# A pooling-mixer layer on one core: one product of the second input phase computed as seven products

## The chip, the cores and the metric

One Trainium2 chip, one of its cores. The metric is the device time of one execution in microseconds (us), measured on that core. Before the change three runs gave 906.58, 906.6 and 907.85 us; the median is 906.6.

Engines as the profile names them: PE is TensorE (matmuls), PEld its weight loads, DVE is VectorE, ACT is ScalarE, POOL is GpSimd, SP is SyncE, which issues most DMAs.

## What is computed

One layer of a streaming trunk on 4096 frames of 1024 channels, in float32:

```python
def pool_mixer(h, in_w, group_w, group_b, scale, out_w):
    b, s, _ = h.shape
    u, gate = jnp.split(h @ in_w, 2, axis=-1)
    ug = u.reshape(b, s, POOL_GROUPS, POOL_GROUP_DIM)
    pooled = jnp.stack([trailing_mean(ug[:, :, g], w) for g, w in enumerate(POOL_WINDOWS)],
                       axis=2) - ug
    mixed = jnp.einsum('bsgc,gcd->bsgd', pooled, group_w) + group_b
    y = mixed.reshape(b, s, POOL_WIDTH) * scale * jax.nn.silu(gate)
    return y @ out_w

normed = rms_norm(h, norm_w[i])
h = h + pool_mixer(normed, pool_in_w[j], pool_group_w[j], ...)
return rms_norm(h, final_norm_w)
```

The four trailing windows are 2, 4, 8 and 16 frames. Nearly all of the work is two matrix products, 4096 x 1024 by 1024 x 2048 (input) and 4096 x 1024 by 1024 x 1024 (output). The group maps are multiplied into the input weights at the start.

## The kernel before

**Products by seven.** Each large product is cut in 2 x 2 blocks and done as seven block products instead of eight (the Strassen-Winograd form). The seven are called P1 to P7. P1, P2 use blocks as they are; P3 to P7 use sums and differences of blocks. Shared partial results stay in PSUM: the eight banks are two sets of four, `x` (banks 0 to 3, also called `v`) and `y` (banks 4 to 7). `bank_of` says which product adds into which set: P1, P2, P7, P4 into `x`/`v`, P6, P5, P3 into `y`.

**Three matmuls for one.** Float32 precision is had from three matmuls of a reduced type: every operand is split in a high part (a copy by ScalarE) and a low part (a subtraction by VectorE, `split`), and `mm3` (line 689) multiplies high by high, high by low and low by high.

**Phases.** The order of products is the list `steps`: the first input phase ("a", 4 blocks of 1024 frames x 7 products) makes one half of the input channels, the second ("b", again 4 x 7) the other half, the out phase ("o", 8 blocks of 512 frames x 7 smaller products) the output. An input product (`product_in`) is 2 x 4 x 2 x 3 = 48 matmuls of 512 columns, with the weights as stationary and the tokens as moving operand. Order in "b": P1, P2, P6, P7, P5, P4, P3. In the out phase eleven products (blocks 2 to 7 of P2, 2 to 6 of P4) are already done as seven products of half the size each (`inner_first`, `inner_rest`, matmuls of 256 columns at line 824, quarter sums added by VectorE at line 832, copies of a quarter bank by ScalarE); their sums of weights come from `inner_rights`, their sums of tokens from `inner_sums`.

**What happens around a product.** The loop at the end goes through `steps`. For step n it loads the blocks of step n + 3 (`load_reach`), forms sums for step n + 2 (`form`), splits the operands of step n + 1 into the four `op` tiles (`split_step`), runs pooling that is due (`pool_due`), and then runs the product and empties its banks (`run`, `evict_in`). The instructions of one engine are put in an order that need not be that of the code: an instruction whose inputs come late lets later ones past it, unless `issue_after` ties it. Emptying in phase "b": P1 is copied to the `y` banks, P2, P6, P7 and P3 are copied to SBUF by ScalarE, P5 and P4 are added there by VectorE. Where two of the four results of a block are there (after P4, after P3), `pool_later` puts the pooling of two channel groups on a list, one or two steps on; it is VectorE work (scans at line 916, scaling and subtraction at 938, bias and gate at 943 and 946) with a store to DRAM (`yd`) at its end.

**Tiles.** Work tiles are 11 `st` and 8 `vt` tiles of 512 KB. A released tile goes to the end of a free list and the oldest is taken; `keep` is the number of `vt` tiles held back for results. When blocks can be loaded depends on when these tiles come free.

**Names that the change touches.** `store_weights` / `inner_rights` / `make_wo` prepare output weights during blocks 1 and 2 of "b"; `split_wb` splits the "b" weights into `w[P3]` and so on (P3's behind block 0's P2); `split_in` splits a product's token blocks; `evict_in` empties its banks; `pool`, `pool_later`, `pool_due` do the pooling.

Of the kernel before, what the change touches and what calls it, by code (L numbers as in the profile page):

```python
# [2 lines left out]

# [7 lines left out]
F32 = mybir.dt.float32  # L11
F32R = mybir.dt.float32r
# [3 lines left out]
P = 128  # L16
# [13 lines left out]
FIRST_INNER = 2  # L30
INNER = {2: (2, 7), 4: (2, 6)}

P1, P2, P3, P4, P5, P6, P7 = range(1, 8)
# [5 lines left out]
class Slots:  # L39
# [41 lines left out]
    def retire(self):  # L81
        return self.free.popleft()[1]


@with_exitstack
def kernel(
# [51 lines left out]
    def new_st(i):  # L138
# [4 lines left out]
    st = Slots([new_st(i) for i in range(NS)])  # L143
    vt = Slots(
        [mem.tile([P, 2 * (HIST + H)], F32, tag=f"vt{i}", name=f"vt{i}") for i in range(NV)]
    )

# [164 lines left out]
    def store_weights(dst, h, b11, b21, b12, b22):  # L312
        nc.sync.dma_start(out=dst[P1][h], in_=b11)
        nc.sync.dma_start(out=dst[P2][h], in_=b21)
        if P2 in firsts:
            inner_rights(P2, b21)
        for i, u in combine(b11, b21, b12, b22).items():
            nc.sync.dma_start(out=dst[i][h], in_=u)
            if i in firsts:
                inner_rights(i, u)  # L320
            give(u)
# [58 lines left out]
    def split_wb(i):  # L380
        for h in range(2):
            (u,) = parts.pop((i, h)).values()
            if i == P1:
                split_scaled(w[i][h], u, pair(norm_c, h, 0))
            elif i == P2:
                split_scaled(w[i][h], u, pair(norm_c, h, 1))
            else:
                split(w[i][h], u)
            if i != P6:
                give(u)  # L390

    QW = H // 4

    def inner_rights(i, low):

        high = firsts.pop(i)
        more = take()
        b11, b12, b21, b22, t4, t2 = (
            u.rearrange("p k (s a) -> p k s a", s=2)[:, :, :, c * QW : (c + 1) * QW] for u in (high, low, more) for c in range(2)
        )  # L400
        sub(b11, b12, b11)
        sub(b12, b22, b12)
        sub(t2, b22, b11)
        sub(t4, b21, t2)
        for n, u in enumerate((high, more)):
            nc.sync.dma_start(out=wid[i][n], in_=u)
            give(u)

    firsts = {}

    def make_wo(h):
        if h:
            for i in INNER:
                firsts[i] = take()
                nc.sync.dma_start(out=firsts[i], in_=wod[i][0])
# [232 lines left out]
    def split_in(q, b, i):  # L648
# [8 lines left out]
        if i == P6 and swapped(q, b):  # L657
            for u in s.pop("21"):
                give(u)
        elif i not in (P1, P2, P6) and not (i == P7 and swapped(q, b)):  # L660
            for u in s.pop(key):
                give(u)
        return t

    stores = []
# [29 lines left out]
    def product_in(i, t, sets, by_bank, between=None, behind=None):  # L695
# [17 lines left out]
        if between and 8 in between:  # L713
            between[8]()

    def product_out(i, t, sets, last, between=None):
# [164 lines left out]

    def pool(b, q, half, vs, sgs):

        first = b == 0 and half == 1
        last = b == NB - 1 and half == 0
        end = HIST + H
        for g in range(2):
            grp = 2 * q + g
# [43 lines left out]
            if win > 2:  # L932
                if first:
# [21 lines left out]
            if not q:  # L955
                give(sg)
        if q:
# [12 lines left out]
    def evict_in(b, q, i, sets):  # L970
# [322 lines left out]
    def run(n, between=None, behind=None):  # L1293
# [12 lines left out]
        else:  # L1306
            product_in(i, split_up.pop(n), sets, i == P1 and n > 0, between, behind)
            evict_in(b, 0 if kind == "a" else 1, i, sets)
# [3 lines left out]
    def pool_later(n):  # L1312
# [7 lines left out]
        else:  # L1320
            return
        pending.append((n + wait, args))

# [218 lines left out]
    def load_reach(kind, b, i):  # L1542
        return 3 if kind == "a" and i == P6 else 4 if kind == "o" else 3

# [17 lines left out]

    scales = {}

# [159 lines left out]
```

## Time and profile before

| what | value |
|---|---|
| median of three runs | 906.6 us |
| the profiled execution | 906.77 us |
| its span, first to last instruction | 904.9 us |
| TensorE busy | 897.3 us, 4428 matmuls |
| VectorE busy | 766.6 us, 945 instructions |
| ScalarE busy | 480.6 us, 791 instructions |
| GpSimd busy | 38.0 us |
| mean granted TensorE clock | 0.998 of full |
| moved by DMA | 194.88 MB |

Busy time is the time in which an engine has an instruction at work; starts and lengths in the views are in us from the first instruction. In a row of a group, the numbers behind the bar are busy time, mean ns of one instruction, and idle time ahead of them with what ended it. A busy share is an average over the whole span; what a stage is limited by is read from the chain of waits in that stage.

### The profile page before, as it was taken

The page shows a single profiled execution, that of the slowest core. Times are in us where ns is not written, and L with a number is a line of the kernel's source. Part 1 is how long each engine was busy: PE and PEld are TensorE (multiplying, and loading weights), DVE is VectorE, ACT ScalarE, POOL GpSimd, SP SyncE. Part 2 cuts the span into 40 slices and gives each one's busy share as a digit, 9 for nine tenths or more (in the row PEclk, how much of TensorE's full clock was granted, in tenths as well). Part 3 has the DMA queues.
Part 4 walks back from the last instruction along what each step waited for, and adds up shares of the span by engine and source line. Part 5 has one row for each costly group of instructions (what it writes and reads, how often), then busy time and mean ns, then how long its engine had stood idle before and what let it go on. Part 6 is the DMA issues. An engine that isn't in the chain of part 4 may idle for free.

```text
span 904.9 us, 11891 instructions
## 1 busy us (share of the span) xinstructions
PE 897.3 (99%) x4428; PEld 792.6 (88%) x4428; DVE 766.6 (85%) x945; ACT 480.6 (53%) x791; POOL 38.0 (4%) x73
## 2 busy tenths in 40 slices
PE   9999999999999999999999999999999999999997
PEld 7888888888888888888888888888888998999996
DVE  5899993894998997586689499889999989889897
ACT  6879547447346555245455544754355445355354
POOL 0023201101100000000000000000000000000000
PEclk9999999999999999999999999999999999999999
DMA  9985965756856635016614774954984483584642
GB/s 348 408 318 163 344 214 205 253 192 221 294 207 229 222 133 209 24 47 233 256 46 175 283 283 167 310 178 176 316 275 155 159 314 131 196 271 162 219 186 93
DMA packets 71881, 194.88 MB, mean 215 GB/s; under 512 B 6608, under 2 KB 29008, under 8 KB 71824
## 3 DMA queue, kind: packets, MB, share of 16 engines
q1 hardware_dynamic: 65328, 172.87, 53.4%
q10 hardware_dynamic: 4176, 13.65, 4.0%
q0 software_dynamic: 2320, 7.62, 2.4%
q8 instruction: 34, 0.56, 0.3%
q14 instruction: 23, 0.19, 0.1%
HBM read 124.89 MB, written 69.22 MB: 215 GB/s over the span
## 4 chain that ended last, share of the span: by engine, by line
PE 98%; DVE 1%; ACT 0%; issue 0%; DVEq 0%; ACTq 0%
PE bank L689 89%; PE bank L824 6%; PE bank L472 3%; PE bank L1332 0%; DVE w L188 0%; DVE op L188 0%; DVE st L188 0%; PE bank L538 0%; ACT vt L1143 0%; DVE st L1223 0%; ACT vt L1184 0%; ACT vt L202 0%; ACT columns L1166 0%; DVE st L1195 0%; DVEq L1720 0%
## 5 line engine op out<-in xcount | busy, mean ns | idle before, releaser
L689 PE MATMUL bank<-op,w 128*128 128x512 f32 x2688 | 581.3, 380 | 0.1
L689 PEld LDWEIGHTS bank<-op,w 128*128 128x128 f32 x2688 | 509.2, 190 | 71.7 <-ACT early L202 0.6
L689 PE MATMUL bank<-w,op 128*128 128x512 f32 (+1 forms) x1092 | 237.0, 377 | 0.0
L689 PEld LDWEIGHTS bank<-w,op 128*128 128x128 f32 x1092 | 203.6, 190 | 27.0 <-issue 0.2
L188 DVE TENSOR_TENSOR op<-st,op 128x1024 fp32r<-128x1024 f32 x121 | 147.1, 1220 | 71.7 <-ACT op L202 71.4
L202 ACT ACTIVATE op<-st 128x1024 fp32r<-128x1024 f32 x121 | 126.9, 1052 | 101.5 <-PE bank L689 82.2
L202 ACT ACTIVATE vt<-bank 128x512 f32<-128x512 f32 x100 | 57.0, 593 | 54.3 <-PE bank L689 39.5
L202 ACT ACTIVATE op<-vt 128x1024 fp32r<-128x1024 f32 x56 | 58.5, 1052 | 44.7 <-PE bank L689 26.5
L188 DVE TENSOR_TENSOR op<-vt,op 128x1024 fp32r<-128x1024 f32 x56 | 67.9, 1219 | 6.9 <-ACT op L202 6.7
L202 ACT ACTIVATE bank<-bank 128x512 f32<-128x512 f32 (+1 forms) x70 | 35.7, 512 | 62.6 <-PE bank L689 32.0
L188 DVE TENSOR_TENSOR st<-st,st 128x1024 f32<-128x1024 f32 (+1 forms) x58 | 64.3, 1128 | 3.4 <-ACT st L293 1.2
L1223 DVE TENSOR_TENSOR vt<-bank,vt 128x512 f32<-128x512 f32 x58 | 39.4, 685 | 3.2 <-PE bank L689 3.2
L188 DVE TENSOR_TENSOR st<-st,vt 128x1024 f32<-128x1024 f32 (+1 forms) x37 | 42.0, 1161 | 0.0
L188 DVE TENSOR_TENSOR vt<-bank,vt 128x512 f32<-128x512 f32 x50 | 33.0, 686 | 6.3 <-PE bank L689 6.3
L188 DVE TENSOR_TENSOR vt<-vt,vt 128x1024 f32<-128x1024 f32 (+1 forms) x32 | 36.7, 1151 | 0.2
L824 PE MATMUL bank<-w,op 128*128 128x256 f32 x264 | 36.6, 275 | 0.0
L824 PEld LDWEIGHTS bank<-w,op 128*128 128x128 f32 x264 | 34.7, 192 | 1.2
L916 DVE TENSOR_TENSOR_SCAN vt<-vt,bf 128x512 f32<-128x512 f32 x28 | 34.5, 1271 | 1.1 <-ACT vt L202 1.1
L188 DVE TENSOR_TENSOR w<-st,w 128x1024 fp32r<-128x1024 f32 (+1 forms) x28 | 30.6, 1105 | 5.5 <-ACT w L202 5.4
L202 ACT ACTIVATE w<-st 128x1024 fp32r<-128x1024 f32 (+1 forms) x28 | 26.6, 960 | 15.9 <-PE bank L689 10.8
L202 ACT ACTIVATE st<-bank 128x512 f32<-128x512 f32 x30 | 17.6, 596 | 26.5 <-PE bank L689 17.1
L1077 POOL TENSOR_SCALAR oms<-oss 128x2 f32<-128x2 f32 x14 | 5.2, 370 | 622.3 <-ACT vt L1104 487.6
(125 smaller groups left out, 662.0 us busy)
## 6 DMA issues: line engine op xcount, KB each, us to landing
st<-in_x SPq DMA_DIRECT2D x29, 512.0 KB, 5.1
vt<-in_x SPq DMA_DIRECT2D x28, 512.0 KB, 5.2
st<-sd SPq DMA_DIRECT2D x28, 512.0 KB, 5.1
st<-in_xt SPq DMA_DIRECT2D x27, 512.0 KB, 7.5
sd<-st ACTq DMA_DIRECT2D x21, 512.0 KB, 4.7
out<-vt SPq DMA_DIRECT2D x19, 512.0 KB, 3.3
yd<-vt SPq DMA_DIRECT2D x18, 512.0 KB, 2.7
st<-yd SPq DMA_DIRECT2D x16, 512.0 KB, 5.5
```

What stands on the lines that cost most here:

```text
L188: made.append(nc.vector.tensor_tensor(out=dst, in0=a, in1=b, op=op))
L202: made.append(nc.scalar.activation(dst, src, func, **how))
L472: latest[0] = nc.tensor.matmul(ps2[kk][:, j * 256 : (j + 1) * 256], a[:, kk, 2 * j + t, :], maps if len(pairs) == 1 else woven(maps), star ...
L689: latest[0] = nc.tensor.matmul(ps, a, b, start=start and n == 0, stop=stop and n == 2, skip_group_check=True).ins
L824: latest[0] = nc.tensor.matmul(dst, a[k][x_], b[k][y_], start=start and k + n == 0, stop=k == 1 and n == 2, skip_group_check=True,).ins
L916: nc.vector.tensor_tensor_scan(s[:, j, at:end], v[:, j, at:end], v[:, j, at - win : end - win], sums_of[j] if sums_of else 0.0, ALU.add, A ...
L1077: nc.gpsimd.tensor_scalar(out=ms, in0=ss, scalar1=-0.5 / D, scalar2=-0.5 * EPS, op0=ALU.mult, op1=ALU.add)
L1223: partial["added"] = nc.vector.tensor_tensor(out=dst, in0=src, in1=dst, op=ALU.add).ins
```

## The change

Block 0 of the second input phase does its last product, P3, as seven products of half the size in each direction (`INNER_IN = (0,)`). P3 is weights (A) times tokens (B) and adds into the `y` banks. The parts are A11 B11, A12 B21, S1 T1, S2 T2, S3 T3, S4 B22 and A22 T4, S and T being sums of quarters of A and B. Three of the seven belong to one quarter of the result each and are added in the `y` banks; A11 B11, S2 T2, S3 T3 and S1 T1 are shared between quarters. The shared ones are computed in the `x` banks, which P4, the product ahead, has just left; ScalarE copies a half bank to go on from it, and VectorE adds the finished half banks to the results in SBUF, twelve additions of 256 elements.

```diff
+    def mm_inner_in(left, right, banks_, n, start):
+        a = inner_left_w[left]
+        for c in range(2):
+            for k in range(2):
+                for m, (x_, y_) in enumerate(((0, 0), (0, 1), (1, 0))):
...
+                        latest[0] = nc.tensor.matmul(
+                            quarter_bank(banks_[c], n), a[:, x_, k, c * P : (c + 1) * P],
+                            right[:, y_, k], start=start and k + m == 0,
...
+    def product_inner(t, sets):
+        r, tags = t
+        y, x = sets["y"], sets["x"]
+        in_turn[0] = None
+        mm_inner_in("A22", r["T4"], y[2:4], 0, False)
+        mm_inner_in("A11", r["B11"], x[2:4], 0, True)
+        for c in range(2):
+            copy(quarter_bank(x[c], 0), quarter_bank(x[2 + c], 0))
+        mm_inner_in("A12", r["B21"], y[0:2], 0, False)
+        mm_inner_in("S2", r["T2"], x[0:2], 0, False)
+        for c in range(2):
+            copy(quarter_bank(x[c], 1), quarter_bank(x[c], 0))
+        mm_inner_in("S4", r["B22"], y[0:2], 1, False)
+        mm_inner_in("S3", r["T3"], x[0:2], 1, False)
+        mm_inner_in("S1", r["T1"], x[2:4], 1, True)
+        for tag in tags:
+            restore(tag)
+
+    def add_shared(us, sets):
+        x = sets["x"]
...
+        for c in range(2):
+            into(c, 1, quarter_bank(x[c], 0))
+        for c in range(2):
+            for n in range(2):
+                latest_add = into(2 + c, n, quarter_bank(x[c], 1))
+        drained.append(latest_add)
+        for c in range(2):
+            into(c, 0, quarter_bank(x[2 + c], 0))
+            for m in range(2):
+                into(2 * m + c, 1, quarter_bank(x[2 + c], 1))
```

The sums. `keep_sums` makes the weights' sums behind block 0's P6, from P3's raw weights, which `split_wb` now holds back instead of releasing them. `token_sums` makes those of the tokens when P3's blocks are split, ahead of P4. Each makes four sums of 512 elements and four splits; three splits each go into work tiles taken from the free list (`retyped`), the fourth overwrites an unused quarter of the operand.

```diff
+    def token_sums(t, us):
...
+        sub(b11, b12, b11)
+        sub(b12, b22, b12)
+        sub(b22, b22, b11)
+        sub(b21, b21, b22)
...
+        for m, src in (("T4", b21), ("T2", b22), ("T3", b12), ("T1", b11)):
+            if m == "T4":
+                dst = whole[0][..., P:]
+            else:
+                tag, dst = retyped()
...
+            split(dst, src)
...
+    def keep_sums(us):
...
+        for m, src in (("S2", a11), ("S1", a22), ("S3", a21), ("S4", a12)):
+            if m == "S4":
+                r[m] = r["A21"]
+            else:
+                tag, dst = retyped()
...
+            split(r[m], src)
+        for u in us:
+            give(u)
```

Emptying and pooling. The `y` banks of the inner product are copied in the order 2, 3, 0, 1, then `add_shared` follows. The pooling that is due in that step is put behind the product instead of ahead of it, and its first group's multiplication is tied behind the add that empties bank 1. The pooling of four products is done in two steps, one group each.

```diff
+PARTED = ((0, 4), (1, 3), (1, 4), (2, 3))
...
-            for c, u in enumerate(cells(ev["12"], HIST)):
-                last = copy(halved(u), plain(ps[c]))
+            inner = is_inner_in(q, b)
+            us = cells(ev["12"], HIST)
+            for c in (2, 3, 0, 1) if inner else range(4):
+                last = copy(halved(us[c]), plain(ps[c]))
+            if inner:
+                add_shared(us, sets)
...
+            if g == 0 and drained:
+                behind.enter_context(tc.issue_after(drained.pop()))
...
-        pending.append((n + wait, args))
+        if kind == "b" and (b, i) in PARTED:
+            pending.append((n + wait, (*args, (0,))))
+            pending.append((n + wait + 1, (*args, (1,))))
+        else:
+            pending.append((n + wait, args))
...
-        pool_due(n)
+        late_pool = kind == "b" and i == P3 and b < NB - 1 and b in INNER_IN
+        if not late_pool:
+            pool_due(n)
...
+        if late_pool:
+            pool_due(n)
```

Loads, tiles and weights. Block 1's P1, P2 and P6 are loaded two steps ahead instead of three. The reserve `keep` of "b" is 3, 4, 4, 4 by block instead of 3, 3, 3, 5. S4 overwrites the quarter A21 of `w[P3]`, so behind the product the raw block is loaded once more, and the quarter is split again behind block 1's P2. The stored halves of two output weights (`firsts`) are loaded in `inner_rights`, where they are used, instead of at the start of `make_wo`.

```diff
-        return 3 if kind == "a" and i == P6 else 4 if kind == "o" else 3
+        return 2 if kind == "b" and b - 1 in INNER_IN and i in (P1, P2, P6) else 4 if kind == "o" else 3
...
-        keep[0] = 0 if kind == "o" and b else 5 if kind == "b" and b == NB - 1 else 3
+        keep[0] = 0 if kind == "o" and b else (3, 4, 4, 4)[b] if kind == "b" else 3
...
+        if kind == "b" and b == INNER_IN[0] and i == P6:
+            with tc.issue_after(latest_split[0]):
+                keep_sums(kept)
+        if kind == "b" and b == INNER_IN[-1] and i == P3:
+            for tag in left_tags:
+                restore(tag)
+            if b < NB - 1:
+                place, lost = wvd[2], take()
+                nc.sync.dma_start(out=lost, in_=place)
+                replaced.append(lost)
+        if replaced and kind == "b" and b == INNER_IN[-1] + 1 and i == P2:
+            lost = replaced.pop()
+            split(inner_left_w["A21"], lost[:, :, 2 * P : 4 * P])
+            give(lost)
...
-        high = firsts.pop(i)
-        more = take()
+        high, more = take(), take()
+        nc.sync.dma_start(out=high, in_=wod[i][0])
```

More of the change, by code (lines that the diff above doesn't have):

```diff
@@ L82, in retire, with restore @@
         return self.free.popleft()[1]
+    def restore(self, t):
+        Slots.clock += 1
+        self.free.append((Slots.clock, t))
 @with_exitstack
@@ L143, with new_vt, retyped, restore @@
     st = Slots([new_st(i) for i in range(NS)])
-    vt = Slots(
-        [mem.tile([P, 2 * (HIST + H)], F32, tag=f"vt{i}", name=f"vt{i}") for i in range(NV)]
-    )
+    def new_vt(i):
+        t = mem.tile([P, 2 * (HIST + H)], F32, tag=f"vt{i}", name=f"vt{i}")
+        st_tag[id(t)] = f"vt{i}"
+        return t
+    vt = Slots([new_vt(i) for i in range(NV)])
+    def retyped():
+        pool = st if st.free else vt
+        t = pool.retire()
+        tag = st_tag[id(t)]
+        u = mem.tile(list(t.shape), F32R, tag=tag, name=f"r{next(names)}_{tag}")
+        return (pool, tag, t.shape), u[:, 0:D]
+    def restore(place):
+        pool, tag, shape = place
+        t = mem.tile(list(shape), F32, tag=tag, name=f"s{next(names)}_{tag}")
+        st_tag[id(t)] = tag
+        pool.restore(t)
+    names = count()
     def unused_w(*products):
@@ L880, in inner_sums, with pool, pool_steps @@
             give(u)
-    def pool(b, q, half, vs, sgs):
+    drained = []
+    def pool(b, q, half, vs, sgs, groups=(0, 1)):
+        with ExitStack() as behind:
+            pool_steps(b, q, half, vs, sgs, groups, behind)
+    def pool_steps(b, q, half, vs, sgs, groups, behind):
         first = b == 0 and half == 1
@@ L886, in pool @@
         end = HIST + H
-        for g in range(2):
+        for g in groups:
             grp = 2 * q + g
@@ L956, in pool @@
                 give(sg)
-        if q:
+        if q and groups[-1]:
             if 2 * b + 1 - half in sumd:
@@ L1306, in run @@
         else:
[L1307 removed]
+            if i == P3 and is_inner_in(kind == "b", b):
+                product_inner(split_up.pop(n), sets)
+            else:
+                product_in(i, split_up.pop(n), sets, i == P1 and n > 0, between, behind)
             evict_in(b, 0 if kind == "a" else 1, i, sets)
```

61 lines of the change are left out of this document (51 added, 10 removed).

## The prediction, on record before the changed kernel ran

> **What bounds the kernel now.** First the page's totals and its chain of waits:
>
> ```profile
> span 904.9 us, 11891 instructions
> ...
> PE 897.3 (99%) x4428; PEld 792.6 (88%) x4428; DVE 766.6 (85%) x945; ACT 480.6 (53%) x791; POOL 38.0 (4%) x73
> ...
> PE 98%; DVE 1%; ACT 0%; issue 0%; DVEq 0%; ACTq 0%
> ```
>
> TensorE is busy 897.3 of 904.9 us and makes up 98% of the chain. The profiled execution took 906.77 us, 1.87 more than its span; the median of the three runs is 906.6, so the sum below is made against 906.77 and 0.17 is taken off at its end. Next the same chain in order of time (start, length, what):
>
> ```profile
> 59.78 639.16 PE bank L689 x2960
> 698.95 0.67 PE bank L824 x6
> 699.62 2.59 PE bank L689 x12
> 702.21 4.02 PE bank L824 x36
> ```
>
> From 59.78 to the last products nothing on the chain is a wait: matmul follows matmul. So the stage of the change, like all others up to the tail, is limited by the number and width of its matmuls, and another engine counts only where it comes late. The rows give both prices: 512 columns wide, 639.16 / 2960 = 0.2159 us from one matmul to the next; 256 wide (the out phase's products that are already done as seven) 4.02 / 36 = 0.1117.
>
> Where the product lies, from the matmuls of the input phases and of the out phase:
>
> ```profile
> L689 PE MATMUL bank<-op,w x2688: 378/380/485, 31.3 to 613.1; 128*128 128x512 f32 x192
> L689 PE MATMUL bank<-w,op x1092: 273/380/411, 613.3 to 898.0; 128*128 128x512 f32 x178, 128*128 128x256 f32 x4
> ```
>
> 2688 are 56 products of 48, each 48 x 0.2159 = 10.37 us. Block 0's P3 of the second input phase is followed by 21 more before 613.3, so it starts 22 x 10.365 earlier, at 385.3, and ends at 395.6. Its neighbours, product by product from block 0's P7 (354.3) to block 1's P6 (416.4):
>
> ```profile
> 354.30:364.70 10.40, 10.40 (x50) 9.14 (x49) 2.45 (x2) 4.40 (x6) 0.00 (x0) 1.00 0.32 115
> 364.70:375.00 10.30, 10.30 (x49) 9.05 (x48) 5.11 (x6) 2.60 (x3) 0.00 (x0) 1.00 0.01 2
> 375.00:385.30 10.30, 10.30 (x49) 9.06 (x48) 7.17 (x9) 3.17 (x3) 0.00 (x0) 1.00 0.00 0
> 385.30:395.70 10.40, 10.40 (x50) 9.14 (x49) 9.95 (x14) 5.11 (x8) 0.00 (x0) 1.00 0.01 2
> 395.70:406.00 10.30, 10.30 (x49) 9.04 (x48) 7.71 (x9) 4.30 (x6) 0.00 (x0) 1.00 0.25 102
> 406.00:416.40 10.40, 10.40 (x50) 9.14 (x49) 9.71 (x9) 7.78 (x23) 0.00 (x0) 1.00 0.41 151
> 416.40:426.80 10.40, 10.40 (x49) 9.12 (x49) 5.49 (x5) 3.00 (x5) 0.00 (x0) 1.00 0.85 299
> ```
>
> The columns are stretch, length, busy time of PE, PEld, DVE, ACT, POOL, clock, DMA share, GB/s. TensorE is full, at full clock. VectorE idles 7.95, 5.19 and 3.13 us ahead of the product (16.3 together), 0.45 in it, and 3.9 in the 31 us behind it.
>
> **Part 1, the matmuls.** Removed: 48 of 512 columns, 10.37 us. Added: seven products of 2 bank columns x 2 row groups x 3 terms = 84 of 256 columns. No row shows this very product, but the out phase's sevenths have its width, its three terms and a weight load for each matmul, so I take their 0.1117: 9.38 us. **Gain 0.98 us.** The price lies between half of 0.2159 (0.108: gain 1.30) and, were each weight load to be waited for, the load itself:
>
> ```profile
> L824 PEld LDWEIGHTS bank<-w,op x264: 188/192/193, 698.6 to 881.6; 128*128 128x128 f32 x132
> ```
>
> 84 x 0.192 = 16.1, a loss of 5.8; but these loads already run beside matmuls 0.1117 apart, so the near end decides.
>
> The Trainium skill ("TensorE: Matmul & The Clock Gate", Back-to-back issue gap) speaks against the change: it says that weight loads and matmuls set the spacing together, and states sustained figures of about 81 ns at 128 columns and 131 at 512. An estimate on a line between them, 98 ns at 256, makes the old product 6.3 us and the new one 8.2, a loss of 1.9. By this rule it would be slower; the rows' 215.9 and 111.7 do not agree with it, and I go by the rows.
>
> **Part 2, VectorE and ScalarE.** Prices (mean ns behind the bar):
>
> ```profile
> L188 DVE TENSOR_TENSOR op<-st,op 128x1024 fp32r<-128x1024 f32 x121 | 147.1, 1220 | 71.7 <-ACT op L202 71.4
> L188 DVE TENSOR_TENSOR st<-st,st 128x512 f32<-128x512 f32 x10 | 6.9, 686 | 1.0 <-ACT st L293 1.0
> L832 DVE TENSOR_TENSOR vt<-bank,vt 128x256 f32<-128x256 f32 x42 | 15.8, 418 | 6.2 <-PE bank L824 6.2
> L202 ACT ACTIVATE op<-st 128x1024 fp32r<-128x1024 f32 x121 | 126.9, 1052 | 101.5 <-PE bank L689 82.2 <-DVE st L188 14.9 <-issue 2.9
> L202 ACT ACTIVATE bank<-bank 128x256 f32<-128x256 f32 x22 | 8.1, 368 | 30.6 <-PE bank L824 16.4 <-DVE vt L1223 11.2 <-DVE st L1223 3.0
> ```
>
> Weight sums (behind block 0's P6, so from about 354): 4 sums and 4 splits of 512 elements, 8 x 0.686 = 5.5 us of VectorE, under the 7.95 idle us of the first row: nothing on the path. Token sums: the same 5.5. They begin when P3's blocks are split, early in P4 (375.0), and have to give T4 by 385.3. VectorE idles 3.13 us there, and two steps of 1.22 that form block 1's sums move behind the product with the loads of Part 4: 5.6 us of room for 5.5, with T4 first among the splits; T2, T3 and T1 are wanted only from 389.3 on. Adds: 12 of 256 elements, 0.33 apart (the row of 706.33 below: (1.42 - 0.42) / 3), 4 us, while VectorE has 0.45 idle us in the product and 3.9 behind: they push pooling and the next splits back by some 4 us, with the 2.4 moved and 0.7 for the weight block that is split again, until the 4.8 idle us of the row 416.4 and those after it take it up. The new wait among them, P4's first pooled group multiplied only after the add that empties bank 1, holds the rest of the pooling and its store on the SP queue; no matmul of this phase reads them. ScalarE's nine 512-element copies (between 0.37 and 1.05 each; 0.6 by the number of elements) and four bank copies of 0.37 are 7 us against 26 idle ones from 354 to 395.7: nothing. Without that cover, 0.37 for each bank copy would be on the path.
>
> **Part 3, the new waits.** The order inside the product leaves one product of 1.34 us between each two that share a bank. What the same order does in the out phase:
>
> ```profile
> 702.71 0.83 PE L824 MATMUL bank<-inner_T,op 128*128 128x256 f32 x6
> ...
> 705.39 0.83 PE L824 MATMUL bank<-inner_T,op 128*128 128x256 f32 x6
> ```
> ```profile
> 703.58 0.37 ACT L202 ACTIVATE bank<-bank 128x256 f32<-128x256 f32 x1 [0.49 <-PE bank L824]
> ```
> ```profile
> 706.33 1.42 DVE L832 TENSOR_TENSOR vt<-bank,vt 128x256 f32<-128x256 f32 x4 [0.99 <-PE bank L824]
> ```
>
> A bank can be read 0.87 to 0.94 us after the first of its six matmuls starts. In the new product (starts 385.3, 386.6, 388.0, 389.3, 390.7, 392.0, 393.3, end 394.7) the first copies are ready at 387.5 and 388.1 and needed at 389.3 and 390.0; the second pair at 390.2 and 390.9, needed at 392.0 and 392.7. Each takes 0.37, so 1.4 us are spare, more than one ScalarE copy of 1.05 in the way.
>
> Tighter are two places of VectorE. A11 B11 starts in P4's banks 2 and 3 at 386.6 and 387.3, which VectorE empties last:
>
> ```profile
> 384.94 1.31 DVE L188 TENSOR_TENSOR vt<-bank,vt 128x512 f32<-128x512 f32 x2
> ...
> 389.11 3.45 DVE L916 TENSOR_TENSOR_SCAN vt<-vt 128x512 f32<-128x512 f32 x3
> ```
>
> done at 386.25: before, these banks were next wanted at 395.6, now 1 us later. And block 1's P1 starts in bank 0 at 394.7, where three adds have to be through: bank 0 is complete at 392.9, three adds take 1.1, so 394.0; 0.7 us spare. An operation of 1.2 us in front costs up to 0.5; I put 0.1 into the sum.
>
> That fourfold add began only at 706.33, though the sum that its first add reads was complete with the six of 702.71. The Trainium skill ("PSUM — Partial Sum Buffer", PSUM bank collisions raise a hardware error) says to guard by bank, not by address; by address one add of the three could go earlier and 1.0 us would be spare. The row agrees with the bank.
>
> **Part 4, tiles, loads and the rest.** The 19 work tiles lend three to the weight sums from 354 and three to the token sums. Followed through the free lists, block 1's P1 blocks still come in by 365; P2's go into the tiles of the token blocks (free about 383); P6's four into tiles of six sums, the last free with the last matmul at 394.7. Before, all were in long ago:
>
> ```profile
> 348.27 14.06 SPq L601 DMA_DIRECT2D st<-sd  x5
> ```
> ```profile
> st<-sd SPq DMA_DIRECT2D x8, 512.0 KB, 4.2
> ```
> ```profile
> 404.99 1.06 ACT L202 ACTIVATE op<-st 128x1024 fp32r<-128x1024 f32 x1 [0.65 <-PE bank L689]
> ```
>
> With 4.2 us to landing they come at about 399, the two subtractions at 401.5, the split at 404.99 waits for its operand buffer anyway, and P6 starts at 415: 10 us of cover, nothing. The SP queue has one more 512 KB load (the weight block that S4 overwrote) behind the loads of P2, in a stretch of 1 to 25% DMA share, needed 60 us later. Pooling in two steps, other reserves of tiles and the later loads of two stored weight halves move work of blocks 1 to 3 by a product, none of it onto TensorE; block 2's P7, ahead of which the stored halves were fetched and near which they are used, has this row:
>
> ```profile
> 499.10:509.50 10.40, 10.40 (x50) 9.13 (x49) 3.15 (x3) 5.52 (x8) 0.00 (x0) 1.00 0.87 311
> ```
>
> 7 us of VectorE to spare; a queue held for one landing (4 us) costs nothing, without cover 4. **Sum:** 906.77 - 0.98 + 0.1 = 905.9; 0.17 off for the median: **905.7**.
>
> **Rivals.** (a) *Given back later.* P3 of the out phase's first block starts at 613.3 + 6 x 24 x 0.2159 = 644.4 in a bank that VectorE frees at 644.18:
>
> ```profile
> 643.49 0.69 DVE L1223 TENSOR_TENSOR st<-bank,st 128x512 f32<-128x512 f32 x1
> ```
> ```profile
> 639.00:644.20 5.20, 5.20 (x26) 4.52 (x24) 5.20 (x7) 0.00 (x0) 0.00 (x0) 1.00 0.81 283
> ```
>
> VectorE is full there and 0.2 us ahead. If its work does not begin earlier with TensorE's, 0.8 of the 0.98 come back as a wait: 906.5. Against it: its work ahead follows matmuls, which all come sooner.
>
> (b) *The bank drain turns into a queue, slower.* At 394.7 VectorE has more ready than one operation: the pooling of P4 (from 389.11 before, put behind the product now), two splits. If a group's two scans, its scaling and a split (4 x 1.2) stand ahead of the three adds, TensorE waits about 4.8 - 0.7 = 4.1 us: 906.6 - 0.98 + 4.1 = 909.7. It decides from a wait of 0.98 (no gain), and for 0.2% from 2.8. For it: 9.95 busy us of 10.40 in the product even now. Against it: the adds come ahead of the pooling in the code.
>
> (c) *Weight loads set the pace* of narrow matmuls: +5.8, 912.4. The L824 rows speak against it.
>
> (d) *Faster by more*: 1.30 from the lowest price gives 905.3; beyond that something else would have to shorten, for which no row speaks.
>
> **Chances.** Forecast 0.69, (a) 0.11, (b) 0.15 with its milder forms, (c) 0.01, (d) 0.04. 0.2% (1.8 us) is about what a measurement of this kernel can tell from no change: forecast and (a) lie within it, and 0.02 of (b). Faster 0.04, same 0.82, slower 0.14. The range goes from 904.9 (the lowest price, and 0.4 for the chip) to 908.8, the waits of (b) up to 3.2 us.
>
> **What would show it.** 84 matmuls of 256 columns 0.11 us apart in one run of 9.4 us at 385; the out phase's first matmul at 612.3 instead of 613.3 (its start tells what the input phases kept); no idle TensorE at bank 2 near 386.6 or bank 0 near 394.7; VectorE full to about 420. A gap ahead of block 1's P1 makes (b) right; 612.3 there with a late end makes (a) right; wider spacing makes Part 1 wrong.

## The result and the profile after

The kernel after the change takes **911.3 us** (median of six runs, 908.5 to 912.7) against 906.5 before on the same chip: ratio 1.0049, interval 1.0038 to 1.0059. The forecast was 905.7 with a range up to 908.8. It is slower, by 4.8 us, and 2.5 us outside the range.

The profiled execution took 911.05 us. Its page begins:

```profile
span 909.3 us, 12004 instructions
...
PE 896.5 (99%) x4464; PEld 790.1 (87%) x4464; DVE 782.1 (86%) x974; ACT 484.4 (53%) x804; POOL 37.4 (4%) x73
```

TensorE is busy 0.8 us less than before, as the change wants it, and VectorE 15.5 us more in 29 more instructions. Yet the span is 4.4 us longer: TensorE now waits. The chain of waits around the new product (start, length, what):

```profile
379.80 5.18 PE bank L772 x24
384.98 9.39 PE bank L805 x84
394.38 0.02 issue
394.39 0.32 SPq L626
394.71 0.04 issue
394.76 5.82 DMA s_st<-sd
```

The 84 matmuls (line 805) are there, in 9.39 us and without a gap. But the chain, which before was TensorE alone from 59.78 on, leaves TensorE at 394.38. It comes back only here (the same view, from the load that it passes last, with the pieces between left out):

```profile
582.65 0.62 DVE vt L215
583.28 0.32 SPq L1013
583.69 5.92 DMA st<-wod
...
646.66 0.61 DVE s_st L1372
647.28 0.14 issue
647.41 7.79 PE bank L772 x35
```

Between 394.38 and 647.41 no piece of the chain is a matmul: it goes through VectorE, here and there ScalarE, and through loads into work tiles that come free late. TensorE's own timeline, and that of before at the start of the out phase, show what was won until there and what was lost:

```profile
611.76 1.46 PE L772 MATMUL bank<-w,op 128*128 128x512 f32 x6
```
```profile
613.28 1.89 PE L689 MATMUL bank<-w,op 128*128 128x512 f32 x8
```
```profile
635.01 10.63 PE L772 MATMUL bank<-w,op 128*128 128x512 f32 x48 [2.37 <-DVE s_st L1372]
647.41 2.83 PE L772 MATMUL bank<-w,op 128*128 128x512 f32 x12 [1.77 <-DVE s_st L1372]
```

The first row is of after, the second of before: the out phase begins 1.52 us earlier. Of that 0.54 is no gain (the steady run of matmuls began at 59.24 instead of 59.78; in the profiled executions of this study it began between 59.08 and 59.91), so **0.98 us** is the product's, to the digit of the forecast. Then TensorE stands twice, 4.1 us together, for an eviction of VectorE (line 1372): P5 and P3 of the out phase's first block wait for banks. The last matmul starts at 901.37 instead of 897.98, and from there to the end of the span it is 7.9 instead of 6.9 us, 1.0 more, to which the experiments come back.

Why VectorE is late, in windows (columns as in the prediction); before, then after:

```profile
0.00:541.00 541.00, 540.07 (x2540) 472.46 (x2541) 434.59 (x465) 303.06 (x488) 32.85 (x59) 1.00 0.61 221
541.00:600.00 59.00, 59.00 (x275) 51.84 (x274) 54.46 (x55) 33.99 (x53) 0.00 (x0) 1.00 0.68 240
600.00:653.00 53.00, 53.00 (x247) 46.45 (x246) 49.91 (x55) 21.66 (x45) 0.00 (x0) 1.00 0.61 212
```
```profile
0.00:541.00 541.00, 540.07 (x2583) 472.26 (x2584) 449.11 (x493) 307.89 (x501) 31.97 (x59) 1.00 0.62 222
541.00:600.00 59.00, 59.00 (x275) 51.67 (x274) 49.91 (x50) 32.97 (x53) 0.00 (x0) 1.00 0.63 209
600.00:653.00 53.00, 48.86 (x226) 42.18 (x225) 52.38 (x56) 18.87 (x42) 0.00 (x0) 1.00 0.66 224
```

Up to 541 VectorE has started 493 instructions in the changed kernel and 465 before. All 29 new ones lie before that point, so it is one instruction of the old work behind. From 541 to 600 it has 50 at work instead of 55 and idles 4.5 us more (49.91 busy instead of 54.46). The timelines of SyncE, ScalarE and VectorE in the changed kernel show where:

```profile
579.08 0.33 SPq L1095 DMA_DIRECT2D yd<-st  x1
580.22 0.37 SPq L1161 DMA_DIRECT2D st<-yd  x1
581.54 2.06 SPq L1013 DMA_DIRECT2D sumd<-vt  x2
583.69 1.43 SPq L451 DMA_DIRECT2D st<-wod  x2
```
```profile
578.94 0.62 ACT L229 ACTIVATE vt<-bank 128x512 f32<-128x512 f32 x1
589.63 1.06 ACT L229 ACTIVATE w<-st 128x1024 fp32r<-128x1024 f32 x1 [10.07 <-DMA st<-wod]
```
```profile
582.57 0.69 DVE L215 TENSOR_TENSOR vt<-st,vt 128x512 f32<-128x512 f32 x1
...
584.30 1.22 DVE L215 TENSOR_TENSOR op<-st,op 128x1024 fp32r<-128x1024 f32 x1
590.72 1.22 DVE L215 TENSOR_TENSOR w<-st,w 128x1024 fp32r<-128x1024 f32 x1 [5.20 <-ACT w L229]
```

Half 0 of P7's output weight (`st<-wod`) is to be split for the out phase. Its tile was that of a gate of block 2, which the pooling's second group (put off by one product in the change) reads last in the operation at 582.57 on VectorE; the load stands on SP's queue behind that group's stores, starts at 583.69 and lands at 589.61. ScalarE stands 10.07 us ahead of the split with evictions queued behind it, and VectorE 5.20.

### The profile page after: what moved, and what is told of

Same layout as the page of the kernel before. It is cut to its first block, busy times and chain, and to the rows that moved or that the text cites. A ratio compares the mean times of both kernels' runs of the same rounds, so it can differ in the third digit from the quotient of the medians.

```text
span 909.3 us, 12004 instructions
## 1 busy us (share of the span) xinstructions
PE 896.5 (99%) x4464; PEld 790.1 (87%) x4464; DVE 782.1 (86%) x974; ACT 484.4 (53%) x804; POOL 37.4 (4%) x73
## 4 chain that ended last, share of the span: by engine, by line
PE 70%; DVE 16%; DMA 7%; issue 4%; ACT 3%; SPq 0%; DVEq 0%; ACTq 0%
PE bank L772 60%; PE bank L961 6%; DVE vt L1059 4%; DVE op L215 3%; PE bank L497 3%; DVE st L215 2%; DVE vt L215 2%; DVE vt L1081 2%; DVE w L215 1%; DMA s_st<-sd 1%; DVE s_st L215 1%; DMA st<-wod 1%; PE bank L805 1%; DMA st<-in_out_w 1%; DMA s_st<-in_out_w 1%
## 5 line engine op out<-in xcount | busy, mean ns | idle before, releaser
L772 PE MATMUL bank<-op,w 128*128 128x512 f32 x2640 | 571.1, 379 | 0.1
L772 PEld LDWEIGHTS bank<-op,w 128*128 128x128 f32 x2640 | 498.5, 189 | 71.9 <-ACT early L229 0.6
L215 DVE TENSOR_TENSOR op<-st,op 128x1024 fp32r<-128x1024 f32 (+1 forms) x88 | 106.1, 1211 | 35.2 <-ACT op L229 35.1
L229 ACT ACTIVATE op<-st 128x1024 fp32r<-128x1024 f32 (+1 forms) x88 | 91.8, 1047 | 60.8 <-PE bank L772 47.5
L229 ACT ACTIVATE vt<-bank 128x512 f32<-128x512 f32 x94 | 52.9, 590 | 42.3 <-PE bank L772 28.3
L229 ACT ACTIVATE op<-s_st 128x1024 fp32r<-128x1024 f32 x32 | 33.7, 1055 | 25.0 <-PE bank L772 11.2
L215 DVE TENSOR_TENSOR op<-s_st,op 128x1024 fp32r<-128x1024 f32 x32 | 38.8, 1218 | 5.4 <-ACT op L229 5.4
L215 DVE TENSOR_TENSOR st<-st,vt 128x1024 f32<-128x1024 f32 (+1 forms) x32 | 37.4, 1199 | 0.0
L229 ACT ACTIVATE vt<-vt 128x1024 f32<-128x1024 f32 (+1 forms) x17 | 17.0, 1003 | 29.3 <-DVE vt L215 29.3
L215 DVE TENSOR_TENSOR st<-st,st 128x1024 f32<-128x1024 f32 (+1 forms) x29 | 30.0, 1052 | 2.1 <-DMA st<-wvd 1.5
```

Source lines behind the costliest of these rows:

```text
L215: made.append(nc.vector.tensor_tensor(out=dst, in0=a, in1=b, op=op))
L229: made.append(nc.scalar.activation(dst, src, func, **how))
L772: latest[0] = nc.tensor.matmul(ps, a, b, start=start and n == 0, stop=stop and n == 2, skip_group_check=True).ins
```

## The experiments

Medians are against the kernel before in the same call. Theory A: VectorE has no room in block 3 of the second input phase, and what it idles there for a late tile or load, TensorE waits for at the out phase's start. Rival B: VectorE never works off the extra work of the product (15.5 us). Rival C: the other reserve of tiles in block 3 is the whole cause.

**Undoing one part (e1 to e4).**

```diff
# e1
-PARTED = ((0, 4), (1, 3), (1, 4), (2, 3))
+PARTED = ((0, 4), (1, 3), (1, 4))
# e2
-INNER_IN = (0,)
+INNER_IN = (9,)
...
-            if i == P3:
-                kept.append(u)
-            elif i != P6:
+            if i != P6:
# e3
-(3, 4, 4, 4)[b] if kind == "b"
+(3, 4, 4, 5)[b] if kind == "b"
# e4: as e3, and
-PARTED = ((0, 4), (1, 3), (1, 4), (2, 3))
+PARTED = ((0, 4),)
```

> The changed kernel with block 2's P3 taken out of the list of products whose pooling is done in two steps; nothing else differs. Theory A (a tile comes late): the pooling's second group is put off by a product, the tile of its gate is free only at 582, the load of half 0 of P7's output weight takes that tile and lands at 589.6, ScalarE's queue stands 10.07 us behind it with the evictions of block 3 in it, VectorE falls behind and TensorE waits 4.5 us at the start of the out phase. With both groups in one step the load takes a tile that was free long before: no ScalarE wait above 2 us near 590, no TensorE gap above 0.5 us at 635 and 647, time 905.5 to 907. Rival B (the extra VectorE and ScalarE work of the seven products in block 0 leaves VectorE behind to the end): the gaps stay, 910.5 to 911.5. Rival C (the other reserve of tiles in block 3 alone): as B, 910.5 to 911.5.

> The changed kernel with the product itself as it was before (48 matmuls of 512 columns, no weight sums, no token sums, no twelve adds), but with the pooling in two steps, the reserves of tiles and the later loads of the change kept. Theory A: the load of half 0 of P7's output weight still takes a tile of the late pooling group, ScalarE waits 5 to 10 us near 590, and the product's 0.98 us are missing as well: 909 to 912. Rival B (extra work of the product): 906 to 907, no gap at 635 and 647. Rival C (reserve of tiles): 909 to 912.

> The changed kernel with five tiles instead of four held in reserve in block 3 of the second input phase, as before. The load of half 0 of P1's output weight then takes a tile that is free early, but that of P7's still takes the gate's tile of the late pooling group. Theory A: ScalarE's wait near 560 is gone, the one near 590 stays, the gaps at 635 and 647 stay: 909 to 911.5. Rival B: 910.5 to 911.5. Rival C: both waits gone, 905.5 to 907.

> The changed kernel with only block 0's P4 pooled in two steps and five tiles in reserve in block 3. Theory A: every load of an output weight in block 3 takes a tile that is free early; no ScalarE wait above 2 us at 560 or 590, no TensorE gap at 635 or 647, the input phases end at 611.5 as in the changed kernel: 905 to 906.5. Rival B: 910.5 to 911.5. Rival C: 905 to 907.

Measured: e1 911.25 (ratio 1.0047, 1.0032 to 1.0062), e2 907.73 (1.0010, 1.0000 to 1.0019), e3 913.05 (1.0071, 1.0054 to 1.0088), e4 920.27 (1.0142, 1.0127 to 1.0157), before 906.61. A's forecasts miss all four. B's range for e1 holds and its range for e2 misses by 0.7 us; e3 and e4 lie above every range. C falls with e3: with its reserve undone the kernel is slower still. A's simple form, that one undone edit brings the load's tile back in time, falls too: an edit deals the tiles anew to all that follows, and others come late. In e1 the wait near 590 is gone, but ScalarE waited for other halves of output weights instead, and TensorE again:

```profile
ACT w L229 <- DMA s_st<-wod: 5.8, 1, 5.8
ACT w L229 <- DMA vt<-wod: 4.8, 4, 2.1
```
```profile
PE bank L772 <- DVE st L1372: 1.5, 1, 1.5
PE bank L772 <- DVE vt L1372: 1.4, 2, 1.1
PE bank L772 <- DVE op L215: 1.0, 1, 1.0
```

(The columns are us in total, times, the longest.) e2 has the pooling in two steps, the reserves and the later loads of the stored halves, without the product and what is tied to it. It cost 1.1 us, against a forecast of nothing, and its interval just reaches no change.

**The load, and VectorE's work, by themselves (e5 to e8).**

```diff
# e5, in load_w
-            nc.sync.dma_start(out=u, in_=src[i][h])
+            if (i, h) != (P7, 0):
+                nc.sync.dma_start(out=u, in_=src[i][h])
# e6, in evict_in
-            if inner:
-                add_shared(us, sets)
# e7 (block 2) and e8 (block 3, with (1, 3) in place of (1, 2)), on the kernel before, in form_in
-                sub(s["2"][h], s["22"][h], s["21"][h])
+                for _ in range(3 if (q, b) == (1, 2) else 1):
+                    sub(s["2"][h], s["22"][h], s["21"][h])
```

> The changed kernel without the load of half 0 of P7's output weight in block 3: its split reads what the tile held before, so that the out phase's P7 multiplies other numbers. Nothing else is left out; the split moves up a place on ScalarE and VectorE. Theory A (VectorE has no room in block 3 of the second input phase; what it idles there for a late tile or load, TensorE waits for at the out phase's start): ScalarE's 10.07 us and VectorE's 5.20 us of idle time at 590 go, and of the 4.5 us of gaps at 635 and 647 at most 1.5 stay: 906 to 908.5. Rival B (the product's extra work in block 0 is still being worked off there): the gaps stay, 910.5 to 911.5.

> The changed kernel without the twelve additions of the shared sums in block 0 (the outputs of that product lack them). VectorE has 4 us less to do at 396 to 416. Rival B: what the gaps at 635 and 647 cost falls by these 4 us: 906.5 to 907.5. Theory A: VectorE had caught up with the extra work by 541 anyway; the gaps are set by what it idles for in block 3 and stay unless the order of the instructions there changes: 909.5 to 911.5.

> The kernel before, with the two differences that form P6's operand in block 2 of the second input phase (128x1024, 1.23 us each) computed three times instead of once: 4.9 us more VectorE work, in a place ahead of the 12 us that VectorE idles between 499 and 520. Theory A: absorbed there, 906.3 to 907. Rival B (VectorE never works off what it has more): 909 to 911.

> The kernel before, with the same 4.9 us of repeated VectorE work in block 3 instead of block 2. From there to the out phase's P3 VectorE idles only 7.6 us between 541 and 653. Theory A: the work comes out as a wait of TensorE at 633 to 650, less what of the idle time it fills (some 2 us): 908.5 to 911. If VectorE's idle time there can be filled altogether: 906.3 to 907.

Measured, with 907.17 before: e5 907.11 (ratio 1.0003, 0.9987 to 1.0019), e6 907.36 (1.0004, 0.9993 to 1.0015), e7 909.51 (1.0022, 1.0012 to 1.0032), e8 913.07 (1.0055, 1.0035 to 1.0075).

Taking one 512 KB load away brings back 4 us. In e5 TensorE never waits from 60 us to the tail, although the 29 VectorE instructions are all there. From 260 us on, VectorE's and ScalarE's instructions have the same order as in the changed kernel, but for the one split that no longer waits:

```profile
600.00:700.00 100.00, 100.00 (x468) 87.56 (x467) 96.53 (x128) 48.83 (x94) 2.15 (x4) 1.00 0.65 224
```

That fits A. But e6 brings back 4 us as well, which B expected and A did not: the adds lie on the same chain, some 220 us ahead of the wait. It does not measure them alone, because the order of VectorE's instructions behind them changed too. And e7 shows that VectorE's 12 idle us from 499 to 520 are no room: the work put ahead of them cost 2.3 us where A expected it to be absorbed (906.3 to 907), while VectorE idled there even longer, 21.00 - 7.54 = 13.5 us instead of 21.00 - 8.74 = 12.3:

```profile
499.00:520.00 21.00, 21.00 (x99) 18.46 (x98) 8.74 (x9) 12.02 (x18) 0.00 (x0) 1.00 0.77 280
```
```profile
499.00:520.00 21.00, 21.00 (x99) 18.37 (x99) 7.54 (x8) 12.17 (x19) 0.00 (x0) 1.00 0.77 277
```

The first is before, the second e7. VectorE waits there for ScalarE, and ScalarE for loads of the output weights (6.9 us of it before, 9.7 in e7), so the work ahead was not taken up by the pause. e8 came out above its range, with all of the 4.9 us and a little more; TensorE's wait in e8:

```profile
PE bank L690 <- DVE op L188: 3.5, 1, 3.5
```

So neither theory holds as stated. The chain of the changed kernel gives the better one, **theory E**: from block 1 on, VectorE's work and the landings of loads into reused tiles make a second chain beside TensorE's, in the kernel before already. e7 and e8 measure how far it lies behind TensorE's: by the medians 4.9 us cost 2.3 in block 2 and 5.9 in block 3. TensorE's timelines of e7 and e8 show what of this is a wait:

```profile
573.21 41.49 PE L690 MATMUL bank<-op,w 128*128 128x512 f32 x191 [1.48 <-DVE op L188]
```
```profile
575.66 43.18 PE L690 MATMUL bank<-op,w 128*128 128x512 f32 x191 [3.46 <-DVE op L188]
```

In these executions some 3.4 us of the work at 470 and 1.4 us of that at 552 found room. The rest of e8's loss lies behind its wait: the same 191 matmuls took 1.7 us longer than in e7, and the granted clock from 570 to 580 was 0.83 instead of 1.00. So a long wait cost more than its length. The change put work onto the second chain (block 0) and late loads (to 590).

**Mending the load (e9 to e12).**

```diff
# e9 in short, in load_w (e11: half 0 alone)
+            if (i, h) == (P6, 1):
+                for half in (0, 1):
+                    fetch_w(src, P7, half)
# e10: as e9, and
-(3, 4, 4, 4)[b] if kind == "b"
+(3, 4, 4, 3 if i == P1 else 4)[b] if kind == "b"
# e12 in short: the changed kernel with
+PARTED = ((0, 4),)
+(3, 3, 3, 5)[b] if kind == "b"
+firsts[i] = take()   # and its load, in make_wo, as before the change
```

> The changed kernel whole, with the two halves of P7's output weight fetched one product earlier in block 3, behind P6's halves, into two tiles that are free by 575; what follows takes other tiles by it. Theory A: the late tile of the gate no longer stands ahead of ScalarE's queue, as without the load (e5): no wait above 2 us of ScalarE for P7's halves, the gaps at 635 and 647 at most 1 us together, 905.5 to 907.5. If another load or tile is late in its place, as in e1: 909 to 911.

> As e9, and with three tiles in reserve instead of four while the halves of P1's output weight are fetched in block 3, so that they land in a tile that is free early and VectorE's 1.96 us of idle time at 561 go too. Theory A: 905 to 907, at most 1 us below e9. If VectorE is held by something else there: as e9.

> As e9 with only half 0 of P7's output weight fetched ahead; half 1 now takes the gate's late tile and lands at about 589.6, where half 0 did. Theory A: the wait moves to half 1, whose split stands later in ScalarE's queue, so a part of the 4.5 us stays: 907 to 910. If only half 0 mattered: as e9.

> The product of the change with as little else as it can do with: the reserves of tiles and the early loads of the two stored weight halves as before, and block 0's P4 alone pooled in two steps. The load of half 0 of P7's output weight takes a tile that is free early, as before. Theory A: no long ScalarE wait near 590, and the time is that of before or up to 1 us less: 905.5 to 907.5. Rival B (the product's own 15 us of VectorE work): 909.5 to 911.5.

Measured, with 906.49 before: e9 907.07 (ratio 1.0014, 1.0000 to 1.0029), e10 906.22 (0.9995, 0.9986 to 1.0005), e11 907.13 (1.0013, 0.9997 to 1.0029; its profiled execution, at 910.44, had a wait of 2.4 us), e12 906.67 (1.0000, 0.9991 to 1.0010). In e9 to e11 `fetch_w` takes the tile and issues the load, and `load_w` then splits from it. Fetching P7's halves one product earlier returns 4.2 of the 4.8 us with the whole product in place, though single executions of e9 still took 911.5 and 911.7 us (e5's longest 910.9; those of e10 and e12 907.3 and 907.7). e12 shows that the product's own work needs no wait at all when the loads find early tiles; rival B falls. e12 and e4 differ only in the reserves of blocks 1 and 2 and in the two early loads, and lie 13.5 us apart, each against the kernel before. The waits in e9 were not all gone, though: ScalarE stood for the store of a sum in their place, and 0.6 us over the kernel before are left:

```profile
ACT vt L230 <- DMA sumd<-vt: 7.2, 1, 7.2
```

In e10 the chain is TensorE's again, from 59.70 to the out phase's products by seven:

```profile
59.70 325.74 PE bank L783 x1508
385.45 9.38 PE bank L816 x84
394.83 303.06 PE bank L783 x1404
```

**The longer end (e13 to e15).** In e12 the last matmul comes 1.19 us earlier than before and the span ends only 0.4 earlier. From the last landing of a store to the end it is 0.91 us before and 1.70 after. The records of SyncE's last waits, in us (the first value is the landing):

```
before  903.99 | 904.01 904.08 (drain)
after   907.58 | 907.60 907.67 908.05 908.13 908.20 908.26 908.32 908.38 908.45 (drain)
```

In the traces SyncE ends with one wait for each of eight semaphores, always in the same order, and the landings of the transfers that SyncE and ScalarE issue are signalled on the eight in turn. They issue 368 transfers before, 46 times eight; the change has one more (the weight block that S4 overwrote). So the last store, which lands last, is signalled on the first of the eight instead of the last, and the other waits run after it.

```diff
# e13 (on e10), e15 (on e12)
-                nc.sync.dma_start(out=lost, in_=place)
+                nc.gpsimd.dma_start(out=lost, in_=place)
# e14, on the kernel before
+                nc.sync.dma_start(out=invt, in_=inv_count)
```

> As e10, with the load of the weight block that S4 overwrote issued on POOL's queue instead of SP's; no other instruction moves. Theory D (the closing waits): SP ends with waits for the semaphores of eight queues in a fixed order; transfers are dealt to them in turn, so that one more transfer makes the first of them the last to come, and the others are waited for after it, some 0.1 us each. With that load off the queues the time from the last landing to the end falls from 1.7 to 0.9 us and the time from 906.2 to 905.4. If the end is longer for the shorter product itself: as e10, 906.2.

> The kernel before with one 32 KB table loaded a second time on SP's queue in the middle of the program, into the tile that holds it already; no other instruction moves. Theory D: last landing to end 1.7 instead of 0.9 us, time 907.0 to 907.6, 0.8 us over the kernel before. If the end is longer for the shorter product: 906.5, as before.

> As e12, with the same load on POOL's queue. Theory D: 0.8 us less than e12, 905.7 to 906.1. Otherwise as e12, 906.7.

Measured, with 906.61 before: e13 906.17 (ratio 0.9995, 0.9987 to 1.0004), e14 907.49 (1.0008, 0.9999 to 1.0016), e15 906.33 (0.9999, 0.9989 to 1.0009). The end behaves as theory D says in all three traces: last landing to end 0.91, 1.70 and 0.92 us. e14 is 0.9 us above the kernel before, as expected, its interval touching no change. Each against the kernel before, e13 and e15 lie 0.17 and 0.46 us under e10 and e12 where 0.8 was expected, with runs from 905.0 to 909.4 and 905.2 to 909.9: the trace shows the 0.8, the medians do not settle it. e13 is the best version found, 0.4 us under the kernel before, and no measurable gain.

**Two more loads of the chain (e16, e17).**

```diff
# e16 in short: in make_wo, as before the change (inner_rights takes them from firsts)
+            for i in INNER:
+                firsts[i] = take()
+                nc.sync.dma_start(out=firsts[i], in_=wod[i][0])
# e17
-(3, 4, 4, 4)[b] if kind == "b"
+(3, 4, 4, 3 if i == P1 else 4)[b] if kind == "b"
```

> The changed kernel with the two stored weight halves loaded ahead, where the kernel before loads them, and not where they are used. Theory E (one chain of VectorE and late loads from 394 to 647): the 5.36 us of that load leave the chain, and as P7's half 0 still takes the gate's late tile only a part comes back: 907.5 to 910. If the load at 590 alone decides (theory A in its first form): 910.5 to 911.5.

> The changed kernel with three tiles in reserve instead of four while the halves of P1's output weight are fetched in block 3, and nothing else: half 0 then takes a tile that is free early, instead of that of a sum whose store ends at 556.6. Theory E: 3 to 5 us leave the chain, 906.5 to 909. Theory A in its first form: 910 to 911.5.

Measured, with 906.71 before: e16 914.63 (ratio 1.0087, 1.0072 to 1.0102), e17 908.55 (1.0019, 1.0006 to 1.0031). e17 is as theory E expects: an earlier tile for P1's half 0 alone returns 3.0 us. e16 misses both ranges and is slower than the changed kernel. Its ScalarE waits 11.5 us for one weight half and 9.9 for another:

```profile
ACT w L229 <- DMA s_st<-wod: 12.1, 2, 9.9
ACT w L229 <- DMA st<-wod: 11.5, 1, 11.5
```

Two tiles held a block longer make other loads later. Under this deal of the tiles, the later load of the two stored halves was thus not a loss of its own. What the chain lacks is tiles that are free early, and that depends on the whole deal. Which deal is best stays open.

All profiled executions together: old VectorE instructions started by 600 (the window from 0 to 600, a kernel's extra ones taken off), TensorE's waits for other engines between 60 and 890, and the median against before.

| kernel | VectorE by 600 | TensorE waits, us | time, us |
|---|---|---|---|
| before | 518 | 0 | 0 |
| e10, e12, e13 | 519 | 0 | -0.3, +0.2, -0.4 |
| e15 | 518 | 0.3 | -0.3 |
| e5, e14 | 517 | 0 | -0.1, +0.9 |
| e6, e7, e9, e17 | 516 | 0.7, 1.5, 0.5, 0.4 | +0.2, +2.3, +0.6, +1.8 |
| e1, e2, e11 | 515 | 3.9, 0.8, 2.4 | +4.6, +1.1, +0.6 |
| e8 | 514 | 3.5 | +5.9 |
| after | 513 | 4.1 | +4.8 |
| e3 | 511 | 5.3 | +6.4 |
| e16 | 507 | 5.7 | +7.9 |
| e4 | 505 | 9.6 | +13.7 |

On the whole, the fewer of its old instructions VectorE has done when the out phase nears, the longer TensorE waits, whichever edit is the cause. The table alone does not show which causes which: in e1, e4, e7, e8, e15 and e16 TensorE waited before 600 already, and VectorE's work that follows its matmuls came later with it. In e4, e8 and e16 the time is 2 to 4 us above the waits. In these the granted clock fell after the waits, to 0.77, 0.83 and 0.91 in a stretch of 10 us; in the changed kernel's profiled execution it stayed at 1.00. (The wait of e11 is that of an execution 3.3 us above its median.)

## Why the prediction was wrong

**What bounds the kernel: incomplete.** TensorE's chain was read rightly. That a second chain, of VectorE and reused tiles, ran 1.4 to 3.4 us behind it (e8, e7) was to be seen at one place only, the 0.2 us at 644.18 which rival (a) quotes, and it was not followed back.

**Part 1, the matmuls: right.** 9.39 us for the forecast 9.38, 0.1118 apart. The estimate from the figures of the Trainium skill ("TensorE: Matmul & The Clock Gate", Back-to-back issue gap), weighed there, was a product slower by 1.9 us; the trace does not agree.

**Part 2, VectorE and ScalarE: right in size, incomplete in effect.** 782.1 - 766.6 = 15.5 us for 5.5 + 5.5 + 4 and the block split again. VectorE is full until about 426 and has caught up to one instruction by 541. "Nothing on the path" was wrong for the changed kernel as it stands: the chain runs through this work from 400 on. It was right for the work itself: e10 and e12 do it all without a wait of TensorE. One reading was off without effect: the rows behind the product hold 8.2 idle us of VectorE in 31 us, not 3.9 (3.3 up to 416.4, and 4.9 behind that).

**Part 3, the new waits: right.** No gap at 386.6 nor at 394.7; the 84 matmuls lie on the chain in one piece, and the 0.1 put into the sum was not needed.

**Part 4, tiles, loads and the rest: the step that failed.** It put the reserves, the two-step pooling and the later loads at nothing: they "move work of blocks 1 to 3 by a product, none of it onto TensorE", and "a queue held for one landing (4 us) costs nothing, without cover 4". In their place the runs showed 4.1 us of TensorE's time. The cover was read from one product, 499.10 to 509.50, where VectorE's 7 us of idle time were themselves waits behind loads (e7). The edits dealt the tiles anew to the loads behind them, and the one that decided came 85 us further on, at 583.69, where VectorE idled 4.5 us in 59 before. That the price without cover, 4, is so near is partly luck: the load took 5.92 us, ScalarE stood 10.07 for it and VectorE 5.20.

That the wait goes when P7's load no longer holds up the chain is shown by e5 and e9. It is not the only link: e6 and e17 return 4 and 3 us further upstream. Nor is one edit the cause by itself. The edits without the product cost 1.1 us (e2), the product with the reserves and early loads of before 0.2 (e12), and both together 4.8. That the pooling in two steps made P7's tile late is read from the changed kernel's rows; e1, which undoes it, could not show it since it dealt the other tiles anew.

**Rivals.** (a) named the place, P3's bank at 644, and "VectorE is full there and 0.2 us ahead", and its sign, an earlier out phase with a late end, is what came. But it took only the product's gain as its price (0.8) and not what may come late upstream of a place without room; its "work ahead follows matmuls, which all come sooner" left out the loads. (b), (c) and (d) did not occur. The end of the program, 0.8 us, was in no case.

Read from the starts of the matmuls, the span's 4.4 us are the following. The steady run starts 0.54 earlier, and the product gives 0.98. The two waits cost 4.56, since P3 of the out phase's first block begins 35.65 us behind that phase's start instead of 31.09. Another 0.35 are lost from there to the last matmul, for which no row gives a cause, and 1.0 at the end, of which 0.8 are the semaphores.

## What to carry to other kernels

Where an engine off the path is only just ahead at one place, it has a chain of its own leading there: follow that back through its instructions and through the tiles that its loads wait for, and price every edit upstream at up to its full length, not by idle time of the stretch in which it lies. Idle time that is a wait for a load need not be room. In a kernel whose tiles go round by a free list, list for each later load the tile it now takes and who reads that last, before an edit of tile counts or of their order is put at nothing.

## What the hardware showed besides

The number of transfers alone lengthened the end: one more load on SP's queue moved the last store from the last of eight semaphores to the first, and SyncE's remaining waits took 0.8 us after it (last landing to end 1.68 to 1.70 us in after, e12 and e14, instead of 0.91 in before; 0.91 and 0.92 in e13 and e15, with that load on POOL's queue).

A wait of TensorE can cost more than its length: behind the wait of 3.46 us in e8, 191 matmuls took 43.18 us, where they took 41.49 behind that of 1.48 us in e7, at a granted clock of 0.83 instead of 1.00 from 570 to 580.
